# Low parts of the out-projection's weights on VectorE, and products of zeros ahead of RWKV's products with an inverse

## The chip, the cores and the metric

The kernel runs on one core of one Trainium2 chip, in one launch. The time is device microseconds of one execution of the whole program. The kernel before takes 2244.4 us, the median of 3 runs (2242.67 to 2246.63). Engine names in rows: PE is TensorE's products and PEld its weight loads, DVE is VectorE, ACT is ScalarE, POOL is GpSimd, SP is SyncE, which here only issues transfers.

## What is computed

Two layers of a hybrid mixer over 1280 tokens (256 of context, 1024 of a picture), width 1024. Each layer normalises its input, projects it, runs four mixers on 256 channels each, joins their outputs, projects them back and adds the result, normalised and gated, to the input:

```python
def mixer_layer(h, mod, p, grid, init, need_out):
    shift, scale, gate = jnp.split(mod, 3, axis=-1)
    hn = rmsnorm(h, p['norm_pre']) * (1.0 + scale) + shift
    proj = hn @ p['w_in']
    f_rw, f_s5, f_ssd, f_gla = split_last(proj, [RW_COLS, S5_COLS, SSD_COLS, GLA_COLS])
    ...
    y = jnp.concatenate([y_rw, y_s5, y_ssd, y_gla], axis=-1).astype(h.dtype) @ p['w_out']
    return h + gate * rmsnorm(y, p['norm_post']), states
```

The RWKV mixer is a recurrence in both directions over a 64x64 state per head (4 heads):

```python
def step(S, inp):
    r_t, w_t, k_t, v_t, kk_t, a_t = inp
    sa = jnp.einsum('bhvk,bhk->bhv', S, -kk_t)
    S = S * w_t[:, :, None, :] + sa[..., None] * (kk_t * a_t)[:, :, None, :] + v_t[..., None] * k_t[:, :, None, :]
    y = jnp.einsum('bhvk,bhk->bhv', S, r_t) if need_out else None
    return S, y
```

The S5 mixer is a diagonal complex recurrence; SSD and GLA are chunked linear attention.

## The kernel before

`body` runs two layers. For each it calls `project` (norm, the input projections, GLA and SSD), then `rw` (RWKV, with the jobs of S5 and the last six input projections put in between), then `out_proj`. The context tokens need no output in the second layer.

**RWKV.** The recurrence is done in windows of 128 tokens, 10 windows, two halves of 64 tokens in each, and both directions at once (a unit u is a direction and a pair of heads, two heads side by side on the free axis). Inside a half the dependence of a token on those before it is a triangular system, and its inverse TT is worked out ahead: `rw_inv` solves 32x32 blocks on VectorE (r_N, r_X, r_tp) and joins them by small products on TensorE (pi<-r_DN, r_DT, r_Bb, r_Rb). `rw_chain` is the serial part. In each half it clears a PSUM bank X (px) with a product of zeros (r_z, bf16), adds the products of A with the values and of the state (r_S) with r_AR, copies the upper half of X to r_rs (left columns on VectorE, right ones on ACT, L1374 and L1375), multiplies by the inverse into the bank pu (four products pu<-r_rs,r_TT), copies the result to r_UV, and forms the new state from pu<-r_UV,r_Bt (X2), which VectorE adds to the decayed old state. `rw_out` forms the outputs r_yw, and `rw_final` norms and gates them (r_yt) and writes them to the scratch tensor yd. The five stages of a window stand in the program in the order 3, 2, 4, 1, 0 (`ORDER`), each for another window, and a scheduler that simulates a time line (L1823) sets the order of the instructions on each engine from that. PSUM has 8 banks in this stage: px 2, pb 2, and one each for pu, pi, ps and p (S5). Since pu has a single bank, the product with the inverse, the copy out of it, X2 and the read of X2 follow each other.

**Out-projection.** The weights (8 blocks m of 128 outputs, each 128x1024 in fp32) are split by `split` into a high part, a cast to fp32r on ACT (L1551, o_w0h to o_w7h), and a low part, the rest, by a subtraction (helper `tt`, L342; o_w0l to o_w7l). It goes in 16 halves of 128x512 through a ring of two buffers o_w: SP issues the transfer of a half (L1550), ACT casts it, and the engine named by the last argument (v for VectorE, p for POOL) subtracts; then the buffer is free for the next transfer. The argument is `"pv"[m % 2]` (L1656), so even blocks go to POOL. Then blocks of 256 tokens follow: their inputs o_y come from yd by SP, are split likewise (o_yh, o_yl), and for each pair of m TensorE does 48 products of 128x256 into one bank pj; ACT squares the bank (o_acc, o_sq), VectorE copies it to o_o (L1681), POOL sums the squares, and a norm, the gate (VectorE) and the input o_x (VectorE and POOL in turn) end the block. SP issues o_w, o_y and o_x from one queue, in order.

Of the kernel before, what the change touches and what calls it, by code (L numbers as in the profile page):

```python
# [24 lines left out]
KD = D // 128  # L25
# [218 lines left out]

RN = (3, 2, 10)
NF = 2

WB = (4, 4)
G1 = ("misc gk", "misc gk")
# [8 lines left out]
class K:  # L258
# [1093 lines left out]
    def rw_chain(self, W, S):  # L1352
        nc = self.nc
        A, AR, Bt, TT, UV, PM = [W[n] for n in ("A", "AR", "Bt", "TT", "UV", "PM")]
        w, need = W["w"], W["need"]
        if need:
            yw = W["yw"] = self.R("r_yw", [128, 2, 256], 1)
        hs = [slice(64 * h, 64 * h + 64) for h in range(2)]
        for s in range(2):
            last = w == 9 and s == 1  # L1360
            X = self.P("px").rearrange("p (u f) -> p u f", u=4)
            self.mm(X.rearrange("p u f -> p (u f)"), self.zero[:, 0:128], self.zero, True, False)
            for u in range(4):
                for h in range(2):
                    self.mm(X[0:64, u, hs[h]], A[:, s, u, h, 0:64], UV[:, s, u, hs[h]], False, False)
            if S is not None:
                for u in range(4):
                    ar = AR[:, u // 2, u % 2, s]
                    if need:
                        self.mm(X[:, u], ar.rearrange("p k t -> p (k t)"), S[:, u], False, False)  # L1370
                    else:
                        self.mm(X[0:64, u], ar[:, 0], S[:, u], False, u == 3)
            rs = self.rzero("r_rs", [128, 4, 128], 2)
            nc.vector.tensor_copy(rs[0:64, :, 0:64], X[0:64, :, 0:64])  # L1374
            nc.scalar.copy(rs[64:128, :, 64:128], X[0:64, :, 64:128])  # L1375
            ps = self.P("pu")[0:64].rearrange("p (u v) -> p u v", u=4)
            for u in range(4):
                self.mm(ps[:, u], TT[:, s * 4 + u], rs[:, u])
            nc.vector.tensor_copy(UV[0:64, s, 0:2], ps[:, 0:2])  # L1379
            nc.scalar.copy(UV[0:64, s, 2:4], ps[:, 2:4])  # L1380
            Sn = None
            if not last:
                X2 = self.P("pu").rearrange("p (u f) -> p u f", u=4)
                for u in range(4):
                    self.mm(X2[:, u], Bt[:, s, u], UV[:, s, u])

                Sn = self.rzero("r_S", [128, 4, 128], 2)
                for h in hs:
                    if S is None:
                        nc.vector.tensor_copy(Sn[h, :, h], X2[h, :, h])  # L1390
                    else:
                        self.tt(Sn[h, :, h], S[h, :, h], PM[h, s].unsqueeze(2).to_broadcast([64, 4, 64]), OP.mult, EG["sp"])
                        self.tt(Sn[h, :, h], X2[h, :, h], Sn[h, :, h], OP.add)
            if need:
                for u in range(4):
                    for h in range(2):
                        self.mm(X[64:128, u, hs[h]], A[:, s, u, h, 64:128], UV[:, s, u, hs[h]], False, u == 3 and h == 1)
                for d in range(2):
                    o = yw[64:128, s] if d == 0 else yw[0:64, s]
                    nc.scalar.copy(o, X[64:128, 2 * d:2 * d + 2].rearrange("p u f -> p (u f)"))  # L1400
            S = Sn
        return S
# [23 lines left out]
    def rw_final(self, blocks):  # L1426
# [3 lines left out]
        bs = sorted(blocks)  # L1430
        x = self.R("r_fin", [128, 2, 6, 128], NF)
        for i, b in enumerate(bs):
# [214 lines left out]
    def out_proj(self, l, h, dst, hi=None, lo=None):  # L1647

        nc, mg = self.nc, self.md[l, 1]
        self.where.update({f"o_w{m}{s}": "oa" if m < 4 else "ob" for m in range(8) for s in "hl"}, o_w="oa",  # L1650
                          **{n: "oy" for n in ("o_yh", "o_yl", "o_y")}, **{n: "oo" for n in ("o_o", "o_acc", "o_sq", "o_x")})
        W = []
        for m in range(8):
            W.append([x.rearrange("p (k m) -> p k m", k=KD) for x in self.split("o_w", f"o_w{m}", [128, 1024], 1, self.A["wout"][l, m], "pv"[m % 2])])
        nb = 1 if hi else 2
        for b in (0, 2, 3, 1, 4) if hi else (2, 3, 1, 4):  # L1656
            b0 = b * 256
            j = 1 if b == 0 else 0
            yh, yl = [self.R("o_y" + s, [128, KD, 256], nb, F32R) for s in "hl"]
            for g in range(4):  # L1660
                gs = slice(2 * g, 2 * g + 2)
                y = self.R("o_y", [128, 2, 256], 3)
                nc.sync.dma_start(out=y, in_=self.yd[l][g * 256:(g + 1) * 256, b0:b0 + 256].rearrange("(k p) t -> p k t", p=128))
                nc.scalar.copy(yh[:, gs], y)
                self.tt(yl[:, gs], y, yh[:, gs].bitcast(F32), OP.subtract)
            x = self.R("o_x", [128, KD, 256])
            nc.sync.dma_start(out=x, in_=h[:, b0:b0 + 256].rearrange("(k p) t -> p k t", p=128))
            o = self.R("o_o", [128, KD, 256], 2)
            acc = self.R("o_acc", [128, 2, 256], 2)
            for m in range(0, 8, 2):  # L1670
                ps = self.P("pj")
                for q in range(2):
                    wh, wl = W[m + q]
                    i = 0
                    for w, t in ((wh, yh), (wl, yh), (wh, yl)):
                        for k in range(KD):
                            self.mm(ps[:, q * 256:(q + 1) * 256], w[:, k], t[:, k], i == 0, i == 3 * KD - 1)
                            i += 1
                sq = acc if m == 0 else self.R("o_sq", [128, 2, 256], 2)
                self.act(sq.rearrange("p k t -> p (k t)"), ps, AF.Square)  # L1680
                nc.vector.tensor_copy(o[:, m:m + 2].rearrange("p k t -> p (k t)"), ps)  # L1681
                if m:
                    self.tt(acc, acc, sq, OP.add, "pppv"[m // 2])
            rs = self.norm([acc[:, 0], acc[:, 1]], "pn")
            od = dst(b0, 256).rearrange("(k p) t -> p k t", p=128)
            for m in range(0, 8, 2):
                for q in range(2):
                    self.stt(o[:, m + q], o[:, m + q], mg[:, m + q, j:j + 1], rs, OP.mult, OP.mult)
                self.tt(o[:, m:m + 2], o[:, m:m + 2], x[:, m:m + 2], OP.add, RA[m // 2])
                if m % 4 == 2:  # L1690
                    nc.sync.dma_start(out=od[:, m - 2:m + 2], in_=o[:, m - 2:m + 2])
            if hi:
                md = self.md[l + 1, 0]
                acc = self.R("o_acc", [128, 2, 256], 2)
                for m in range(0, 8, 2):
                    sq = acc if m == 0 else self.R("o_sq", [128, 2, 256], 2)
                    self.act(sq, o[:, m:m + 2], AF.Square)
                    if m:
                        self.tt(acc, acc, sq, OP.add, AA[m // 2])
                rs = self.norm([acc[:, 0], acc[:, 1]], "pn")  # L1700
                bb = 0 if b == 0 else (b + 1) // 2
                t = b0 - BLK[bb][0]
                for k in range(KD):
                    self.stt(o[:, k], o[:, k], md[:, 8 + k, j:j + 1], rs, OP.mult, OP.mult)
                    ho, lw = [v[bb][:, k, t:t + 256] for v in (hi, lo)]
                    self.act(ho, o[:, k], AF.Identity, bias=md[:, k, j:j + 1])
                    self.stt(lw, o[:, k], md[:, k, j:j + 1], ho.bitcast(F32), OP.add, OP.subtract)
# [119 lines left out]
```

## Time and profile before

| What | Value |
| --- | --- |
| Median of 3 runs | 2244.4 us (2242.67 to 2246.63) |
| Profiled execution | 2243.13 us |
| Its span (first to last instruction) | 2241.4 us |
| Mean granted clock of TensorE | 0.926 of full speed |
| RWKV, layer 0 | 700 to 1045 us of the span |
| RWKV, layer 1 | 1757 to 2085 us |
| RWKV's last rows and out-projection, layer 0 | 1045 to some 1210 us |
| RWKV's last rows and out-projection, layer 1 | 2085 us to the end |

The profile is one execution, and the rows below are of it; its time is 1.3 us below the median of the runs. Busy shares are of the whole span and hide that the stages differ: a window of the trace is read for itself. [...]

### The profile page before, as it was taken

Reading aid. Unit: us, or ns where it says so; the run is one execution under the profiler, and the core shown is the slowest. Engines: PE = TensorE matmul, PEld = TensorE weight load, DVE = VectorE, ACT = ScalarE, POOL = GpSimd, SP = SyncE. Lnnn points to the kernel's source line nnn. Section 1 sums busy time; section 2 is a strip of 40 time slices with the busy share of each in tenths; the row PEclk is TensorE's granted clock in tenths of the full one; section 3 lists DMA queues with packets and bytes.
Section 4 is the critical chain, followed back from the end, with each engine's and each line's share of the span. In section 5 each row is a group of like instructions: output and inputs, shape, how many; then the busy total and the mean of one; then the engine's idle time right before and its main releaser. Section 6 shows DMA issues by size and latency. Waiting matters only on the chain. (4 is left out here: it accounts for less than half of the span.)

```text
span 2241.4 us, 45148 instructions
## 1 busy us (share of the span) xinstructions
PE 1947.4 (87%) x17712; PEld 1664.7 (74%) x17712; DVE 1529.2 (68%) x3423; ACT 916.7 (41%) x2009; POOL 846.5 (38%) x965
## 2 busy tenths in 40 slices
PE   6777999999997887878799779999999787889697
PEld 4667889678886676765799667887888676676497
DVE  3877646794146888885377786677754899896344
ACT  2434314333256447632233544234335755544220
POOL 0446460342024455532322255522332454542222
PEclk9889999999998888979999899999999989889698
DMA  7234425434633222214333335242234232212332
GB/s 247 74 118 132 157 83 170 128 115 133 187 99 116 88 74 81 70 40 140 90 114 113 120 125 175 89 145 80 70 112 125 98 105 68 86 47 73 122 104 95
DMA packets 204021, 246.83 MB, mean 110 GB/s; under 512 B 28384, under 2 KB 145632, under 8 KB 203808
## 3 DMA queue, kind: packets, MB, share of 16 engines
q1 hardware_dynamic: 169936, 213.13, 30.6%
q10 hardware_dynamic: 33008, 28.45, 3.9%
q8 instruction: 139, 2.28, 0.4%
q0 software_dynamic: 864, 2.36, 0.3%
q14 instruction: 74, 0.61, 0.1%
HBM read 169.27 MB, written 76.71 MB: 110 GB/s over the span
## 5 line engine op out<-in xcount | busy, mean ns | idle before, releaser
L330 PE MATMUL pj<-hi,i_wh 128*128 128x512 f32 (+1 forms) x696 | 180.2, 379 | 18.3 <-DVE hi L1528 13.2
L330 PE MATMUL pj<-lo,i_wh 128*128 128x512 f32 (+1 forms) x696 | 176.9, 372 | 0.1
L330 PE MATMUL pj<-hi,i_wl 128*128 128x512 f32 (+1 forms) x696 | 174.3, 368 | 2.7 <-DVE i_wl L342 2.7
L342 DVE TENSOR_TENSOR i_wl<-i_w,i_wh 128x512 fp32r<-128x512 f32 x108 | 84.8, 791 | 107.6 <-ACT i_wh L1551 37.6
L330 PEld LDWEIGHTS pj<-hi,i_wh 128*128 128x128 f32 x696 | 124.2, 199 | 43.1 <-DVE hi L1528 13.4
L330 PEld LDWEIGHTS pj<-hi,i_wl 128*128 128x128 f32 x696 | 123.9, 195 | 25.6 <-DVE i_wl L342 3.2
L330 PEld LDWEIGHTS pj<-lo,i_wh 128*128 128x128 f32 x696 | 124.0, 197 | 22.6 <-issue 2.6
L330 PE MATMUL px<-r_UV,r_A 128*64 128x64 f32 x1216 | 108.2, 247 | 17.0 <-DVE r_UV L1379 9.8
L330 PEld LDWEIGHTS px<-r_UV,r_A 128*64 128x64 f32 x1216 | 92.6, 157 | 37.5 <-DVE r_UV L1379 13.9
L1551 ACT CAST i_wh<-i_w 128x512 fp32r<-128x512 f32 x108 | 66.0, 620 | 122.0 <-PE pj L330 80.8
L1289 DVE TENSOR_TENSOR r_X<-r_X,r_tp 128x30 f32<-128x30 f32 (+1 forms) x300 | 93.8, 313 | 8.0
L342 DVE TENSOR_TENSOR r_tp<-r_N,r_X 128x30 f32<-128x30 f32 (+1 forms) x300 | 90.5, 302 | 7.2
L330 PE MATMUL pb<-r_AD,r_BK 128*128 128x256 f32 x320 | 85.2, 407 | 5.5 <-POOL r_BK L342 3.6
L342 POOL TENSOR_TENSOR r_S<-r_S,r_PM 64x256 f32<-64x256 f32 x72 | 54.0, 750 | 79.0 <-DVE r_S L342 66.8
L342 DVE TENSOR_TENSOR r_A<-pb,rcon 128x512 f32<-128x512 f32 x80 | 53.5, 682 | 42.2 <-PE pb L330 41.9
L330 PEld LDWEIGHTS pb<-r_AD,r_BK 128*128 128x128 f32 x320 | 60.9, 201 | 17.1 <-POOL r_BK L342 3.9
L330 PE MATMUL pj<-i_wh,hi 128*128 128x256 f32 x448 | 71.0, 296 | 2.9 <-ACT i_wh L1551 1.5
L345 POOL TENSOR_SCALAR r_AD<-r_AR 64x512 f32<-64x512 f32 (+1 forms) x80 | 54.4, 680 | 48.9 <-PE pb L330 42.4
L330 PE MATMUL pu<-r_rs,r_TT 128*64 128x128 f32 x320 | 49.2, 303 | 21.1 <-ACT r_rs L1375 20.8
L342 POOL TENSOR_TENSOR o_o<-o_o,o_x 128x512 f32<-128x512 f32 x18 | 23.8, 1323 | 114.7 <-DVE o_o L348 113.5
L330 PE MATMUL pj<-i_wl,hi 128*128 128x256 f32 x448 | 66.8, 289 | 0.2 <-DVE i_wl L342 0.2
L330 PEld LDWEIGHTS pj<-i_wh,hi 128*128 128x128 f32 x448 | 61.4, 198 | 6.7 <-issue 2.7
(469 smaller groups left out, 5445.9 us busy)
## 6 DMA issues: line engine op xcount, KB each, us to landing
i_w<-in_win SPq DMA_DIRECT2D x108, 256.0 KB, 3.0
r_in<-rm SPq DMA_DIRECT2D x36, 512.0 KB, 4.5
a_w<-in_ada SPq DMA_DIRECT2D x64, 256.0 KB, 3.8
rm<-i_o SPq DMA_DIRECT2D x48, 256.0 KB, 2.5
o_y<-yd SPq DMA_DIRECT2D x36, 256.0 KB, 3.0
i_o<-in_ada SPq DMA_DIRECT2D x32, 256.0 KB, 4.6
z_st<-s5t SPq DMA_DIRECT2D x32, 256.0 KB, 2.7
o_w<-in_wout SPq DMA_DIRECT2D x32, 256.0 KB, 2.7
```

The costliest lines, as they stand in the source:

```text
L330: self.nc.tensor.matmul(out, lhsT, rhs, start=start, stop=stop, skip_group_check=True)
L342: (self.nc.vector if e == "v" else self.nc.gpsimd).tensor_tensor(out, a, b, op)
L345: (self.nc.vector if e == "v" else self.nc.gpsimd).tensor_scalar(out, a, s1, s2, op0, op1)
L1289: last = nc.vector.tensor_tensor(X[:, :, :i, r0:4], X[:, :, :i, r0:4], tmp[:, :, :i, r0:], OP.add)
L1551: self.nc.scalar.copy(hi[:, v], w)
```

## The change

It does two things. The call of `split` in `out_proj` loses its last argument, so that all low parts of the out-projection's weights go to `split`'s default engine, VectorE: 8 more subtractions of 128x512 in each layer (o_w0l, o_w2l, o_w4l and o_w6l, two halves each). In `rw_chain`, four products of zeros (the bf16 tile r_z as weights and as 512 columns) are written into the bank of pu ahead of the four products with the inverse, each of which begins a new sum, so that nothing of the zeros is left. There are 20 halves in each layer, so 160 such products, each with its load of weights.

```diff
--- before.py
+++ after.py
@@ -244,6 +244,8 @@
 
 RN = (3, 2, 10)
 NF = 2
+
+FILL = 4
 
 WB = (4, 4)
 G1 = ("misc gk", "misc gk")
@@ -1373,7 +1375,11 @@
             rs = self.rzero("r_rs", [128, 4, 128], 2)
             nc.vector.tensor_copy(rs[0:64, :, 0:64], X[0:64, :, 0:64])
             nc.scalar.copy(rs[64:128, :, 64:128], X[0:64, :, 64:128])
-            ps = self.P("pu")[0:64].rearrange("p (u v) -> p u v", u=4)
+            bank = self.P("pu")
+
+            for _ in range(FILL):
+                self.mm(bank, self.zero[:, 0:128], self.zero)
+            ps = bank[0:64].rearrange("p (u v) -> p u v", u=4)
             for u in range(4):
                 self.mm(ps[:, u], TT[:, s * 4 + u], rs[:, u])
             nc.vector.tensor_copy(UV[0:64, s, 0:2], ps[:, 0:2])
@@ -1651,7 +1657,7 @@
                           **{n: "oy" for n in ("o_yh", "o_yl", "o_y")}, **{n: "oo" for n in ("o_o", "o_acc", "o_sq", "o_x")})
         W = []
         for m in range(8):
-            W.append([x.rearrange("p (k m) -> p k m", k=KD) for x in self.split("o_w", f"o_w{m}", [128, 1024], 1, self.A["wout"][l, m], "pv"[m % 2])])
+            W.append([x.rearrange("p (k m) -> p k m", k=KD) for x in self.split("o_w", f"o_w{m}", [128, 1024], 1, self.A["wout"][l, m])])
         nb = 1 if hi else 2
         for b in (0, 2, 3, 1, 4) if hi else (2, 3, 1, 4):
             b0 = b * 256
```

The lines of the kernel after stand 2 to 6 lower. The scheduler puts many other instructions of the RWKV stages in another order. Three places follow.

On TensorE, in the second half of a window in layer 0 (r_S is the state, r_AR what it is multiplied by, r_AD, r_BK, r_DN and r_Am belong to the next window's blocks and inverse, z_ and p_ to S5; a number behind a name is its buffer's). Before:

```order
L330 MATMUL px<-r_S_7029,r_AR_8211 128x128 x4
L330 MATMUL pi<-r_DN,r_Am 32x32 x24
L1263 MATMUL pb<-con,r_BK 128x128 x8
L330 LDWEIGHTS r_z
L330 MATMUL px<-r_z 128x512
L330 MATMUL ps<-rcon,r_yw 128x128 x2
L330 MATMUL p_9891<-z_us,z_st 128x160 x3
L330 MATMUL pu<-r_rs_7012,r_TT_6837 64x128 x4
```

After:

```order
L332 MATMUL px<-r_S_7033,r_AR_8235 128x128 x4
L332 LDWEIGHTS r_z
L332 MATMUL pu<-r_z 128x512
...
L332 LDWEIGHTS r_z
L332 MATMUL pu<-r_z 128x512
L332 LDWEIGHTS r_z
L332 MATMUL px<-r_z 128x512
L332 MATMUL ps<-rcon,r_yw 128x128 x2
L332 MATMUL pb<-r_AD_6322,r_BK 128x256 x4
...
L332 MATMUL pi<-r_DN,r_Am 32x32 x8
L332 MATMUL pu<-r_rs_7012,r_TT_6837 64x128 x4
```

The four zeros into pu come right after the state's product, and other work that stood between the state's product and the product with the inverse is now partly behind it.

On VectorE, at the end of RWKV and the start of the out-projection in layer 1 (r_yt are RWKV's gated outputs). Before:

```order
L348 SCALAR_TENSOR_TENSOR r_yt<-r_yt,par,r_ks_18041 128x2x128 x2
L342 TENSOR_TENSOR o_w1l<-o_w,o_w1h 128x512 x2
L342 TENSOR_TENSOR o_w3l<-o_w,o_w3h 128x512
L1681 COPY o_o<-pj 128x512
L342 TENSOR_TENSOR o_w3l<-o_w,o_w3h 128x512
L1681 COPY o_o<-pj 128x512
L342 TENSOR_TENSOR o_w5l<-o_w,o_w5h 128x512 x2
```

After:

```order
L350 SCALAR_TENSOR_TENSOR r_yt<-r_yt,par,r_ks_18121 128x2x128 x2
L344 TENSOR_TENSOR o_w0l<-o_w,o_w0h 128x512 x2
L344 TENSOR_TENSOR o_w1l<-o_w,o_w1h 128x512 x2
L1687 COPY o_o<-pj 128x512
L344 TENSOR_TENSOR o_w2l<-o_w,o_w2h 128x512 x2
L344 TENSOR_TENSOR o_w3l<-o_w,o_w3h 128x512 x2
L344 TENSOR_TENSOR o_w4l<-o_w,o_w4h 128x512 x2
L1687 COPY o_o<-pj 128x512
L344 TENSOR_TENSOR o_w5l<-o_w,o_w5h 128x512 x2
```

o_w0l stands directly behind r_yt, and o_w2l and o_w4l behind the copies out of pj. In layer 0 the order is o_w0l, o_w1l, the first half of o_w2l, a copy out of pj, its second half, and so on by turns.

On ACT, the same place in layer 1 (o_acc<-pj is the Square of the first two blocks of outputs). Before:

```order
L1551 CAST o_w0h<-o_w 128x512 x2
L1551 CAST o_w1h<-o_w 128x512 x2
L1551 CAST o_w2h<-o_w 128x512 x2
L1551 CAST o_w3h<-o_w 128x512
L339 ACTIVATE o_acc<-pj 128x512
L1551 CAST o_w3h<-o_w 128x512
```

After:

```order
L1557 CAST o_w0h<-o_w 128x512 x2
L1557 CAST o_w1h<-o_w 128x512 x2
L341 ACTIVATE o_acc<-pj 128x512
L1557 CAST o_w2h<-o_w 128x512 x2
L1557 CAST o_w3h<-o_w 128x512 x2
```

The Square now stands ahead of both casts of o_w2h, and before it stood between the casts of o_w3h.

## Rows read from the trace of the kernel before

**Rows 1.** The page, busy time, share of the span and instructions of each engine:

```profile
PE 1947.4 (87%) x17712; PEld 1664.7 (74%) x17712; DVE 1529.2 (68%) x3423; ACT 916.7 (41%) x2009; POOL 846.5 (38%) x965
```

**Rows 2.** Windows, RWKV stages: stretch, us, busy (instructions) by engine, clock, DMA, GB/s:

```profile
700.00:1045.00 345.00, 284.15 (x3488) 237.14 (x3487) 290.89 (x647) 180.40 (x433) 159.82 (x213) 0.88 0.27 85
1757.00:2085.00 328.00, 271.36 (x3412) 224.92 (x3412) 282.37 (x635) 176.57 (x428) 158.16 (x211) 0.90 0.27 82
```

**Rows 3.** Windows, layer 0's 13 stretches at the low clock, one and their sum:

```profile
815.00:819.00 4.00, 3.49 (x16) 3.16 (x17) 3.90 (x11) 2.09 (x6) 1.93 (x3) 0.57 0.00 0
...
sum 80.00, PE 65.72 PEld 55.50 DVE 66.53 ACT 30.69 POOL 23.45; mean PE 5.06 PEld 4.27 DVE 5.12 ACT 2.36 POOL 1.80
```

**Rows 4.** Windows, the 13 such stretches of layer 1, their sum:

```profile
sum 61.00, PE 54.92 PEld 46.63 DVE 50.85 ACT 18.33 POOL 19.73; mean PE 4.22 PEld 3.59 DVE 3.91 ACT 1.41 POOL 1.52
```

**Rows 5.** Windows, the 4 us ahead of the one stretch shown:

```profile
811.00:815.00 4.00, 0.25 (x3) 0.06 (x1) 3.97 (x6) 0.00 (x0) 2.44 (x6) 1.00 0.53 171
```

**Rows 6.** Chain of waits, 2100 to 2145 us: start, us, what:

```profile
2107.16 1.68 DVE r_yt L348 x4
...
2112.00 2.30 POOL o_w0l L342 x2
2114.31 4.11 DMA o_w<-in_wout
...
2123.37 0.63 ACT o_w2h L1551
...
2124.07 1.29 POOL o_w2l L342
...
2139.54 2.67 DMA o_w<-in_wout
...
2142.98 18.90 PE pj L330 x144
```

**Rows 7.** Tile o_w: duration in ns min/median/max, first and last start, forms:

```profile
L342 DVE TENSOR_TENSOR o_w1l<-o_w,o_w1h x4: 692/693/693, 1076.4 to 2123.3; 128x512 fp32r<-128x512 f32 x4
...
L342 DVE TENSOR_TENSOR o_w7l<-o_w,o_w7h x4: 676/780/1340, 1102.5 to 2149.9; 128x512 fp32r<-128x512 f32 x4
```

**Rows 8.** Timeline, layer 0's out-projection: start, us, engine, what [idle before <-releaser]:

```profile
1067.73 0.88 DVE L348 SCALAR_TENSOR_TENSOR r_yt<-r_yt,par,r_ks 128x256 f32<-128x256 f32 x2
1068.74 1.26 POOL L342 TENSOR_TENSOR r_yt<-r_yt,r_fin 128x512 f32<-128x512 f32 x1 [8.09 <-DVE r_yt L348]
...
1071.79 2.50 POOL L342 TENSOR_TENSOR o_w0l<-o_w,o_w0h 128x512 fp32r<-128x512 f32 x2
1073.09 1.55 SPq L1550 DMA_DIRECT2D o_w<-in_wout  x2
...
1104.27 0.62 ACT L1551 CAST o_w7h<-o_w 128x512 fp32r<-128x512 f32 x1 [1.85 <-DMA o_w<-in_wout]
```

**Rows 9.** Timeline, SP in layer 1's out-projection:

```profile
2112.81 1.40 SPq L1663 DMA_DIRECT2D o_y<-yd  x3
...
2115.29 0.53 SPq L1550 DMA_DIRECT2D o_w<-in_wout  x1
```

**Rows 10.** Timeline, TensorE: products of zeros and the next, full and low clock:

```profile
1876.90 0.38 PE L330 MATMUL px<-r_z 128*128 128x512 bf16 x1
1877.12 0.61 PE L330 MATMUL ps<-rcon,r_yw 128*128 128x128 f32 x4
...
1998.77 0.63 PE L330 MATMUL px<-r_z 128*128 128x512 bf16 x1
1999.19 0.93 PE L330 MATMUL ps<-rcon,r_yw 128*128 128x128 f32 x4
```

**Rows 11.** Tile r_rs: engines idle before its instructions until (us, times):

```profile
  ACT r_rs L1375: 45.0, 30
```

**Rows 12.** Timeline, TensorE: products with an inverse:

```profile
815.51 1.97 PE L330 MATMUL pu<-r_rs,r_TT 128*64 128x128 f32 x8 [4.26 <-ACT r_rs L1375]
...
2059.14 1.09 PE L330 MATMUL pu<-r_rs,r_TT 128*64 128x128 f32 x8
```

## The prediction

> **What bounds the kernel now.** I read the busy shares first, then the busy time of the two RWKV stretches by windows, then the chain of waits. Over the whole span TensorE is the busiest engine, 87% [rows 1], but that mean hides two kinds of stage. In the RWKV stages (700 to 1045 us in layer 0, 1757 to 2085 us in layer 1, 673 us together) VectorE is the fuller one, 290.89 of 345 and 282.37 of 328 us, and TensorE's granted clock is 0.88 and 0.90 [rows 2]. There the reader is to see what VectorE does where the clock is low. I marked the pieces, to 1 us, in which the clock stood at its lower level: 13 in layer 0, 80 us together, and 13 in layer 1, 61 us. VectorE is busy for 66.53 us of the 80 and 50.85 of the 61 [rows 3, 4], 83% in both; in the rest of the stretches it is 224.4 of 265 and 231.5 of 267, or 85% and 87%. So a slow TensorE hardly slows VectorE. The other way round it shows: from 811 to 815 VectorE works 3.97 of 4 us and TensorE 0.25, at full clock [rows 5]; the next 4 us are at 0.57 [rows 3]. TensorE waits, and its clock falls.
>
> The second kind of stage is the start of each out-projection. The chain of waits runs there through a ring of two 128x512 buffers for the weights: transfer, cast, low part, next transfer. In layer 1 it passes RWKV's last VectorE rows, then POOL's o_w0l at 2112.00, then transfer by transfer to 2142.98, and from there on only TensorE products [rows 6].
>
> **The low parts.** Sixteen subtractions, eight in each layer, leave POOL for VectorE. One takes 0.69 us there (o_w1l) [rows 7]; on POOL the pair takes 2.50 [rows 8], 1.25 each. What counts first is the start. In layer 0 the casts of o_w0h are long done and VectorE ends r_yt at 1067.73 + 0.88 = 1068.6, but POOL has its own r_yt product and its transfers to issue and begins o_w0l at 1071.79; only after its first half SP issues the next weight transfer, 1073.09 [rows 8]. In the new order o_w0l stands on VectorE right behind r_yt: halves done at about 1069.4 and 1070.1 against 1073.0 and 1074.3, 3.6 and 4.2 us earlier. Then each of o_w2, o_w4 and o_w6 shortens a turn of the ring by 1.29 [rows 6] - 0.69 = 0.60 us, 1.8 us for three. Against this, the second half of o_w2l, o_w4l and o_w6l now stands behind a copy out of PSUM that waits for products and for ACT's Square; with TensorE starting 3.6 us earlier too I price this at 0.5. Layer 0: -4.2 - 1.8 + 0.5 = -5.5 us.
>
> In layer 1 VectorE ends r_yt at 2107.16 + 1.68 = 2108.8 and POOL starts at 2112.00 [rows 6]. The third weight transfer moves ahead of a load of o_y and can go at 2109.6 instead of 2114.31, 4.7 us earlier. The fourth stays behind that o_y, which waits for RWKV's result to land and is issued at 2112.81; so it goes at 2113.3 instead of 2115.29, 2.0 earlier [rows 6, 9]. On ACT the Square of the first two outputs now stands ahead of both casts of o_w2h, and it needs the products of o_w1's second half: 2113.3, a transfer of 2.7 to 4.1 us (2.67 and 4.11 in the chain), cast and low 1.3, some 4 us of products at the low clock, Square 0.6: casts of o_w2h from about 2122.7, against 2123.37 (0.7 earlier). The turns of o_w2 and o_w4 give 0.6 each, and the two halves then come closer together than before: 3 us at o_w6, where TensorE takes over the chain. Layer 1: -3 us.
>
> Both: -8.5 us. The ends are -2.3 and -10.7. The upper one: -6.0 and -4.7, nothing lost behind the copies. The lower one: layer 1 gives nothing, because the Square and the copies eat it (VectorE's queue then holds o_w3l and o_w4l behind a late copy), and layer 0 only its 3.6 less 1.26 for POOL's r_yt product, which runs at the same moment. That overlap has a price in the trace: an o_w7l that runs beside POOL's o_acc takes up to 1.34 us against 0.69 [rows 7].
> [...]
>
> **The products of zeros.** 40 products with an inverse get four products of 128x512 ahead of them, 160 in all, each with its weight load. The trace has the same product (r_z into px): the next one starts 0.22 us later at full clock (1876.90 to 1877.12) and 0.42 at the low one [rows 10]. 160 x 0.22 = 35 us of TensorE time, 67 at the most. Cover: TensorE is idle 117 of the 673 us [rows 2], and 45.0 us of this in front of this very product, in 30 waits for the copies of r_rs [rows 11]. The order puts them only partly there: in the second half of a window they stand between r_S's product and the copies, where they replace other products as filler; in the first half they run before X is made. Their bank is the single pu, free once VectorE has read X2; r_S's product needs that read too, so I add no wait. Ends: 0 and +35 us. VectorE, the pace-setter, idles 99.8 of 673 us, 15%, and only there can TensorE be late for it: 0.15 x 35 = +5.
>
> What they give is the clock. Were the slow pieces cured, VectorE would gain at most its idle time in them, 13.5 + 10.1 = 23.6 us; if only the idle above the usual rate goes, 1.3 + 2.0 = 3.3 us [rows 2 to 4]. I count the pieces that begin within 2 us of the start of such a product: 10 of 26, one at 815 (product at 815.51, after 4.26 us of waiting), the last at 2061 (2059.14) [rows 12]. 10/26 x 23.6 = -9. The other sixteen begin in waits for the 32x32 inverse or for S5, where no zeros stand. So -9 + 5 = -4 us.
>
> The change also puts other RWKV, S5 and second-layer projection products in another order; they are the same instructions, and I count 0 for it, with 8 us to either side (a twelfth of VectorE's idle time).
>
> **Sum.** -8.5 - 4 = -12.5. The profiled execution took 2243.1 us (span 2241.4 and 1.7 around it), so 2230.6; the median of the runs lies 1.3 above it: 2232 us, -0.55%. What is late next in the RWKV stages is VectorE's own work; in the out-projections TensorE from the last weight on.
>
> **Rivals.**
> The zeros hold the clock. For it: in each fall the trace shows TensorE waiting just before [rows 5, 12]. Against: most falls lie where no zeros are put. All slow pieces gone: -23.6 + 5 - 8.5 = -27, 2217 us.
> [...]
>
> The zeros only cost nothing and give nothing. VectorE's equal shares in slow and fast pieces speak for it. -8.5: 2236 us.
>
> Slower: the zeros stand in TensorE's queue, which runs in order, ahead of what VectorE waits for. Place: the first half of a window, where they come ahead of the inverse's products and of the next X. For it: 0.9 us per group at full clock, 1.7 at the low one; against: TensorE's idle time. If half of the 35 us arrives at VectorE and the clock gains nothing, +17.5 - 8.5 = +9, 2253 us; all of it, 2271. It decides from a quarter of the 35 us on.
>
> The low parts don't do what they say: on VectorE they queue behind the copies and beside POOL's products, the ring keeps its pace (-2), and the RWKV stages balance: 2242 to 2244 us.
>
> **How the numbers follow.** Forecast 0.37, clock held 0.17, only the low parts 0.13, slower 0.22, no effect 0.11. The forecast's own range is 2222 to 2242 (its bounds and the 8 us of order). With the rivals to either side, and leaving out 1 in 10 at each end, 2212 to 2256. A measurement of this kernel tells about 0.2%, 4.5 us, from no change. Faster by more: 0.35 of the forecast, 0.17, 0.10 and 0.02, 0.64. Within it: 0.02 + 0.03 + 0.02 + 0.07 = 0.14. Slower: 0.22.
>
> **What would show it.** Right: o_w0l on VectorE within 0.2 us of r_yt's end, the last o_w7h cast in layer 0 some 5 us sooner after r_yt than the 36.5 us of before (1067.73 to 1104.27 [rows 8]); in layer 1 the products taking over about 3 us sooner after r_yt; granted clock 0.92 or more in the RWKV stages with VectorE's busy time unchanged and the stages shorter by a few us. Wrong: a clock near 1.0 with the stages much shorter (the clock did bind); the clock up and the stages as long (VectorE binds alone); waits of VectorE for pu, pi or px that grow (the zeros are in the way); o_w2l waiting for copies so long that the ring is no faster.

## The result and the profile after

The kernel after takes 2258.09 us (median of 5 runs, 2254.97 to 2262.58), the kernel before 2244.4 us (median of 5, 2242.67 to 2249.12). The ratio is 1.0055, 95% interval 1.0037 to 1.0074: 0.55% or some 14 us slower, where 0.55% faster was forecast. The profiled execution took 2262.58 us, 4.5 above its median, so its stages carry a little more than the median's loss.

The page's busy times of the kernel after, as in [rows 1]:

```profile
PE 1985.3 (88%) x17872; PEld 1689.0 (75%) x17872; DVE 1535.1 (68%) x3439; ACT 917.3 (41%) x2009; POOL 821.0 (36%) x949
```

TensorE is busy 38 us longer. For the loss that is a wrong trail, as the experiments show; the next rows say where the time went. They are windows from the first copy of r_rs in a layer to the end of its last r_yt, the RWKV stage without its overlap into the stages beside it (columns as in [rows 2]). First the kernel before:

```profile
704.50:1068.60 364.10, 296.33 (x3556) 245.81 (x3554) 296.64 (x673) 182.91 (x439) 161.44 (x211) 0.87 0.27 83
1761.30:2108.80 347.50, 281.68 (x3440) 231.17 (x3440) 287.99 (x659) 178.67 (x431) 157.79 (x210) 0.88 0.26 80
```

and the kernel after:

```profile
704.70:1086.00 381.30, 315.29 (x3631) 256.03 (x3629) 298.59 (x673) 182.86 (x439) 160.04 (x211) 0.87 0.25 76
1781.50:2130.80 349.30, 294.46 (x3516) 238.70 (x3516) 284.24 (x657) 179.73 (x431) 154.22 (x207) 0.89 0.25 79
```

Layer 0's stage is 17.2 us longer, layer 1's 1.8. VectorE does the same work in both (296.64 and 298.59, 287.99 and 284.24 us); what has grown is the time in which it stands, from 67.5 to 82.7 and from 59.5 to 65.1 us, 20.8 together. The granted clock of the stages is what it was. Where VectorE stands is told by the groups of its instructions (busy, mean ns, then the idle time just before them and what ended it). Before:

```profile
L1278 DVE STREAM_TRANSPOSE r_N<-r_Ad 128x1024 f32<-128x1024 f32 x20 | 39.7, 1985 | 12.3 <-ACT r_Ad L1035 12.2
L342 DVE TENSOR_TENSOR r_S<-pu,r_S 64x256 f32<-64x256 f32 x72 | 30.1, 419 | 11.0 <-PE pu L330 9.8
L1379 DVE COPY r_UV<-pu 64x256 f32<-64x256 f32 x40 | 16.4, 410 | 9.9 <-PE pu L330 9.8
```

After:

```profile
L1280 DVE STREAM_TRANSPOSE r_N<-r_Ad 128x1024 f32<-128x1024 f32 x20 | 39.9, 1995 | 21.4 <-ACT r_Ad L1037 21.3
L344 DVE TENSOR_TENSOR r_S<-pu,r_S 64x256 f32<-64x256 f32 x72 | 30.3, 421 | 24.9 <-PE pu L332 23.6
L1385 DVE COPY r_UV<-pu 64x256 f32<-64x256 f32 x40 | 16.4, 410 | 11.0 <-PE pu L332 10.8
```

The copy r_UV is the first that waits for the product behind the zeros, and its wait hardly grows (9.9 to 11.0 us). The waits that grew stand one step later: the new state r_S (+13.9 us) and the next window's transpose r_N (+9.1). The longest single wait for r_S is in layer 0, in the seventh half. VectorE's timeline there, after:

```profile
824.06 2.44 DVE L344 TENSOR_TENSOR z_x<-z_b,z_t 64x636 f32<-64x636 f32 x3
826.53 0.42 DVE L1385 COPY r_UV<-pu 64x256 f32<-64x256 f32 x1
...
827.32 1.60 DVE L344 TENSOR_TENSOR r_BK<-r_th,r_cs 128x512 f32<-128x512 f32 x1
828.84 0.63 DVE L1311 STREAM_TRANSPOSE r_DN<-r_DT 128x256 f32<-128x256 f32 x1
832.98 0.87 DVE L344 TENSOR_TENSOR r_S<-pu,r_S 64x256 f32<-64x256 f32 x2 [3.50 <-PE pu L332]
```

and the same half before, where the copy r_UV starts at 818.33:

```profile
820.50 2.63 DVE L342 TENSOR_TENSOR z_x<-z_a,z_bb 64x636 f32<-64x636 f32 x3
...
823.68 1.16 DVE L348 SCALAR_TENSOR_TENSOR r_a<-r_a,r_in 128x256 f32<-128x256 f32 x2
824.76 2.43 DVE L342 TENSOR_TENSOR z_x<-z_b,z_t 64x636 f32<-64x636 f32 x3
827.22 0.88 DVE L342 TENSOR_TENSOR r_S<-pu,r_S 64x256 f32<-64x256 f32 x2
```

Before, z_x (S5) and r_a (another window) lie between r_UV and r_S and cover the wait. After, z_x has been done ahead of r_UV, and VectorE runs dry for 3.50 us. The product that r_S waits for has moved too. TensorE there, after:

```profile
826.60 0.87 PE L332 MATMUL p<-z_x,z_st 128*128 128x160 f32 x2 [3.22 <-DVE z_x L344]
...
829.40 1.27 PE L332 MATMUL p<-z_x,z_st 128*128 128x160 f32 x4
830.60 1.12 PE L332 MATMUL px<-r_UV,r_A 128*64 128x64 f32 x8
831.65 1.29 PE L332 MATMUL pu<-r_UV,r_Bt 128*128 128x128 f32 x8
```

and before:

```profile
820.37 1.16 PE L330 MATMUL pu<-r_UV,r_Bt 128*128 128x128 f32 x8 [0.24 <-ACT r_UV L1380]
...
823.23 0.51 PE L330 MATMUL p<-z_x,z_st 128*128 128x160 f32 x2 [1.10 <-DVE z_x L342]
```

S5's products p, which themselves wait for z_x (3.22 us), now stand ahead of the state's product pu<-r_UV,r_Bt and hold it to 831.65; before, it came first. No zeros stand in this piece: it is the same work in another order.

The out-projections, layer 0, timeline of the kernel after (VectorE, POOL, SP, ACT; compare [rows 8]):

```profile
1085.17 0.88 DVE L350 SCALAR_TENSOR_TENSOR r_yt<-r_yt,par,r_ks 128x256 f32<-128x256 f32 x2
1085.96 1.29 DVE L344 TENSOR_TENSOR o_w0l<-o_w,o_w0h 128x512 fp32r<-128x512 f32 x2
...
1086.18 2.22 POOL L344 TENSOR_TENSOR r_yt<-r_yt,r_fin 128x512 f32<-128x512 f32 x1 [8.09 <-DVE r_yt L350]
...
1086.67 0.93 SPq L1556 DMA_DIRECT2D o_w<-in_wout  x2
1087.70 0.38 SPq L1673 DMA_DIRECT2D o_x<-in_hT  x1
1090.90 1.25 SPq L1556 DMA_DIRECT2D o_w<-in_wout  x2
...
1097.26 0.62 ACT L1557 CAST o_w2h<-o_w 128x512 fp32r<-128x512 f32 x1 [6.53 <-DMA o_w<-in_wout]
...
1124.03 0.62 ACT L1557 CAST o_w7h<-o_w 128x512 fp32r<-128x512 f32 x1 [3.61 <-DMA o_w<-in_wout]
```

The start is as forecast: o_w0l right at r_yt's end, the next weights out at 1086.67, 1.5 us behind r_yt's start against 5.4 before. But the 1024 KB of o_x went out long ahead of the ring before:

```profile
1053.99 0.38 SPq L1667 DMA_DIRECT2D o_x<-in_hT  x1
```

Now it goes out at 1087.70, between the weights; the half issued at 1090.90 is cast at 1097.26, 6.4 us later. The last o_w7h stands 38.9 us behind r_yt (36.5 before) in this execution. POOL's r_yt, beside o_w0l, takes 2.22 us against 1.26, 0.96 us more, with 1.07 us of o_w0l still to run at its start.

Layer 1, the chain of waits, after (compare [rows 6]):

```profile
2138.32 9.22 DMA o_w<-in_wout
...
2161.78 8.33 PE pj L332 x66
```

Again a half of the weights, queued behind o_x and two o_y, takes 9.22 us (in this layer o_x stood among the weights before, too, at 2114.77). TensorE takes over 30.9 us behind the last r_yt (which ends at 2130.8; before 34.1), so 3.2 us sooner, about the forecast's 3. How far these two figures carry is seen under e1.

### The profile page after: what moved, and what is told of

It reads as the page before. It is cut to its first block, busy times and chain, and to the rows that moved or that the text cites. A ratio compares the mean times of both kernels' runs of the same rounds, so it can differ in the third digit from the quotient of the medians.

```text
span 2260.6 us, 45461 instructions
## 1 busy us (share of the span) xinstructions
PE 1985.3 (88%) x17872; PEld 1689.0 (75%) x17872; DVE 1535.1 (68%) x3439; ACT 917.3 (41%) x2009; POOL 821.0 (36%) x949
## 5 line engine op out<-in xcount | busy, mean ns | idle before, releaser
L332 PE MATMUL pj<-hi,i_wh 128*128 128x512 f32 (+1 forms) x696 | 180.4, 380 | 16.7 <-DVE hi L1534 13.2
L332 PE MATMUL pj<-hi,i_wl 128*128 128x512 f32 (+1 forms) x696 | 173.8, 366 | 2.7 <-DVE i_wl L344 2.7
L344 DVE TENSOR_TENSOR i_wl<-i_w,i_wh 128x512 fp32r<-128x512 f32 x108 | 90.6, 844 | 112.6 <-ACT i_wh L1557 52.9
L344 DVE TENSOR_TENSOR r_tp<-r_N,r_X 128x30 f32<-128x30 f32 (+1 forms) x300 | 96.3, 321 | 7.3
L344 POOL TENSOR_TENSOR o_acc<-o_acc,o_sq 128x512 f32<-128x512 f32 x23 | 31.1, 1352 | 116.0 <-ACT o_sq L341 115.9
```

The source lines that it names most:

```text
L332: self.nc.tensor.matmul(out, lhsT, rhs, start=start, stop=stop, skip_group_check=True)
L344: (self.nc.vector if e == "v" else self.nc.gpsimd).tensor_tensor(out, a, b, op)
```

## The experiments

All are compared with the kernel before on the same chip. They ask whether the zeros' time costs the 14 us or the new order, what the low parts are worth and why so little, and what makes an order good.

**e1, the low parts alone.**

```diff
- ... self.split("o_w", f"o_w{m}", [128, 1024], 1, self.A["wout"][l, m], "pv"[m % 2]) ...
+ ... self.split("o_w", f"o_w{m}", [128, 1024], 1, self.A["wout"][l, m]) ...
```

> The low parts alone: the kernel before, with o_w0l, o_w2l, o_w4l and o_w6l on VectorE and no products of zeros; RWKV of layer 0 keeps the order of before. Theory A (the recorded sum of the out-projections was right and the loss is all in RWKV): -8.5 us, 2236. Theory B (in the profile after, layer 0's out-projection takes 148.5 us from RWKV's last r_yt on, against 144.4 before, because the new order of SP's queue puts the 1 MB load of o_x at 1087.70 between the halves of the weights, and the o_w issued next takes 6.33 us to land against 2.5 to 2.8 before; layer 1 gains about 3): layer 0 +2 to +4, layer 1 -3, 2242 to 2246, and o_x again among the first weights.

Measured: 2243.78 us (12 runs), ratio 1.0006 (0.9988 to 1.0023). No gain: theory A's -8.5 us lies outside the interval (-3 to +5 us), and no loss is shown either. SP's queue in layer 0, and the chain in layer 1:

```profile
1067.11 0.38 SPq L1667 DMA_DIRECT2D o_x<-in_hT  x1
```

```profile
2115.58 8.92 DMA o_w<-in_wout
...
2143.07 6.94 PE pj L330 x56
```

o_x is again among the first weights. The last o_w7h of layer 0 stands 35.5 us behind r_yt (before 36.5), and in layer 1 TensorE takes over 35.0 us behind it (before 34.1). For the same low parts, the traces of after and e3 have 38.9 and 34.2 in layer 0 and 30.9 and 32.9 in layer 1; for the low parts as before, e2 and e4 have 37.8 and 37.8, and 32.1 and 33.7. From trace to trace each figure moves by 1 to 5 us, so neither the 2.4 us that after loses in layer 0 nor the 3.2 us that it gains in layer 1 is shown to come from the edit.

This edit, too, changes an order: in layer 0's RWKV it is before's, in layer 1's it is another, and that stage is 5.1 us longer in the profile (352.6 against 347.5). So e1 is not the price of the low parts alone.

**e2, the zeros alone,** the kernel after with the low parts put back:

```diff
- ... self.split("o_w", f"o_w{m}", [128, 1024], 1, self.A["wout"][l, m]) ...
+ ... self.split("o_w", f"o_w{m}", [128, 1024], 1, self.A["wout"][l, m], "pv"[m % 2]) ...
```

> The products of zeros alone, four ahead of each product with an inverse, low parts as before; RWKV of layer 0 in the order of after. If the low parts are worth -8.5 us, this is slower than after by so much: 2267. If they are worth about nothing (theory B of the low parts), it is as after: 2256 to 2260, with layer 0's RWKV some 17 us longer than before (368.6 us from 700 to the last r_yt) and layer 1's some 2 us.

Measured: 2256.97 us (6 runs), ratio 1.0062 (1.0042 to 1.0082). The whole loss comes with the edit of the zeros.

**e3, the order of after without the zeros.** A function changes the program after the scheduler has set the order; of each four products one is left (of the 160 in all, 43), and that of one column:

```diff
+ ...
+ if i.outs[0].memref == bank and i.sync_info is None and made[at].sync_info is None:
+     del made[at]          # the load; the product is skipped
+     continue
+ ...
+ i = copy.replace(i, ins=(x, i.ins[1]), outs=(y,))   # x, y: one column of 512
```

> The kernel after with every engine's instructions in its own order, but of each four products of zeros only one is left, and that of one column instead of 512: the order of after without the zeros' time (117 products and their loads fewer). Theory 1 (the zeros' time stands on the path, 160 x 0.22 us = 35 us of TensorE, of which 19 came through): layer 0's RWKV loses its 17 us and the whole is 2240 to 2244. Theory 2 (the new order of RWKV, S5 and projections costs it, and the zeros' time is hidden in TensorE's idle time): within 4 us of after, 2254 to 2260, and a clock somewhat lower than after's 0.922.

Measured: 2260.65 us (6 runs), ratio 1.0071 (1.0049 to 1.0093), as slow as after itself. The zeros' time is not what costs. In the trace every engine has after's order in both RWKV stages. The windows and VectorE's groups of e3:

```profile
705.90:1086.70 380.80, 301.12 (x3576) 249.88 (x3574) 298.86 (x673) 182.58 (x439) 159.69 (x211) 0.87 0.24 76
1780.70:2129.40 348.70, 282.02 (x3460) 234.15 (x3460) 284.18 (x657) 179.14 (x431) 155.06 (x207) 0.86 0.25 79
```

```profile
L1281 DVE STREAM_TRANSPOSE r_N<-r_Ad 128x1024 f32<-128x1024 f32 x20 | 39.9, 1995 | 23.6 <-ACT r_Ad L1038 23.6
L345 DVE TENSOR_TENSOR r_S<-pu,r_S 64x256 f32<-64x256 f32 x72 | 30.2, 420 | 25.6 <-PE pu L333 24.3
L1386 DVE COPY r_UV<-pu 64x256 f32<-64x256 f32 x40 | 16.3, 408 | 8.7 <-PE pu L333 8.5
```

TensorE's busy time is back to 301 and 282 us, and the stages are as long as after's, with the same two waits grown. With the zeros some of the clock goes, too: over the whole span the granted clock is 0.9155 (median of the runs; 0.910 to 0.918), against 0.923 in e2 and in after (0.920 to 0.927). So e3 and e4 price the zeros' time together with the clock that they give.

**e4, the order of before with the zeros,** put in after the order was set:

```diff
+ ...
+ for _ in range(n):      # ahead of the first product with r_rs into a bank
+     made.append(copy.replace(ld, name=nc.get_next_instruction_name(), sync_info=None))
+     made.append(copy.replace(mm, ..., sync_info=None, outs=(o,), stop_tensor_calc=True))
```

> The kernel before with every engine's instructions in its own order, and four products of zeros with their loads put directly ahead of each product with an inverse: the zeros' time without the new order. Theory 1 (the zeros' time): 12 to 20 us slower than before, 2256 to 2264. Theory 2 (the order): within 4 us of before, 2240 to 2248; if the zeros lift the clock and that counts, below 2240.

Measured: 2247.27 us (12 runs), ratio 1.0013 (0.9998 to 1.0027). Theory 2 holds: the zeros in before's order (which the trace shows in both stages) cost 3.5 us at the middle, not told from none. The wait of r_UV, which stands behind them:

```profile
L1380 DVE COPY r_UV<-pu 64x256 f32<-64x256 f32 x40 | 16.4, 410 | 23.2 <-PE pu L331 23.0
```

13 us more than before. This is the longest execution of the 12, 2256.09 us, 8.8 above their median, so the row shows more than the usual price. Its granted clock in the two stages is 0.88 and 0.87, but of the 12 it has the lowest clock over the whole span, and before's profile (0.926) one of the highest of its kernel: the 12 have 0.925 to 0.935 (median 0.930), and the kernel before has 0.917 to 0.927 in 22 of its 23 runs (median of all 0.922). So four products of zeros do lift the clock, by some 0.008 in the mean over the whole span, here and in after's order, and no time is seen to come of it.

**e5, the low parts with o_x late.**

```diff
...
+ with self.tc.issue_after(self.wd.ins):      # wd: the last transfer of o_w
      nc.sync.dma_start(out=x, in_=h[:, b0:b0 + 256].rearrange("(k p) t -> p k t", p=128))
```

> The low parts on VectorE, no zeros, and each block's load of o_x queued on SP behind the last o_w; the order of RWKV is that of the low parts alone. Theory B (the 1 MB of o_x beside the weights ate the gain): in layer 0 the seventh o_w transfer goes out some 9 to 10 us after the last r_yt instead of 12.5, in layer 1 some 14 to 15 instead of 17.9, and the whole is 6 us faster than the low parts alone, 2238. Rival (the ring is held by the copies out of PSUM and the products, not by o_x): 2242 to 2246, with the same issue times as before.

Measured: 2237.13 us (12 runs), ratio 0.9976 (0.9962 to 0.9990): 5.7 us under the kernel before on its chip, where e1 was level with it. In the traces e1 and e5 have the same order of RWKV in both layers. Theory B holds. It is the one version that beats both kernels. SP's queue in layer 0:

```profile
1068.31 29.85 SPq L1550 DMA_DIRECT2D o_w<-in_wout  x14
1098.21 0.43 SPq L1668 DMA_DIRECT2D o_x<-in_hT  x1
```

the last cast of layer 0:

```profile
1100.57 0.62 ACT L1551 CAST o_w7h<-o_w 128x512 fp32r<-128x512 f32 x1 [3.15 <-DMA o_w<-in_wout]
```

and the chain in layer 1:

```profile
2125.60 2.81 DMA o_w<-in_wout
...
2137.57 12.44 PE pj L330 x102
```

The halves of the chain land in 2.6 to 2.8 us from there on, with no 8.92 among them. The last o_w7h of layer 0 stands 33.8 us behind r_yt, and in layer 1 TensorE takes over 27.8 us behind it (2109.8), 3.1 sooner than after and 6.3 sooner than before. Both are below every figure named under e1.

**o6, o5 and o8: other orders, without zeros.** The low parts are as before, and the zeros are taken out as in e3.

```diff
-FILL = 4
+FILL = 6          # o5: 5, o8: 8; o1 and o2 below: 1 and 2
```

> Low parts as before; the order that the scheduler makes with six products of zeros per product with an inverse, and then the zeros taken out as in e3 (one of one column is left). Theory S (what VectorE has queued between its copy of r_UV and r_S sets the time: where it is less than the 3.5 us of the longest wait for r_S in the profile after, VectorE stands; the lack, summed over the 38 places with durations of before's rows, is 19.5 us in before's order and 29.7 in after's, which e3 shows to be 15 us slower, 1.5 us for each us of lack): here the lack is 17.1, so -3.5 us, 2240. Rival (any order other than before's costs some 13 us): 2257.

> As o6, with the order that five products of zeros make. Theory S: the lack is 21.0 us, +2 us, 2246. Rival (any other order costs 13): 2257.

> As o6, with the order that eight products of zeros make. Theory S: the lack is 27.1 us, +11 us, 2255. Rival (any other order costs 13): 2257. A second rival, that the order's cost is a matter of chance and the lack says nothing of it: the three orders stand in another row than 17.1, 21.0, 27.1.

Measured: o6 2286.32 us, ratio 1.0189 (1.0167 to 1.0211); o5 2264.79, 1.0097 (1.0080 to 1.0115); o8 2274.40, 1.0148 (1.0125 to 1.0171). Theory S falls: the order with the least lack is the slowest. What VectorE has queued ahead of r_S is one such place among several: in o6 it stands 13.4 us for r_S and 29.3 for r_N (before 11.0 and 12.3):

```profile
L1281 DVE STREAM_TRANSPOSE r_N<-r_Ad 128x1024 f32<-128x1024 f32 x20 | 39.7, 1987 | 29.3 <-ACT r_Ad L1038 29.3
L345 DVE TENSOR_TENSOR r_S<-pu,r_S 64x256 f32<-64x256 f32 x72 | 30.2, 419 | 13.4 <-PE pu L333 12.1
```

**o1 and o2: the orders of one and two.** Is it the zeros' planned time, or any other order?

> As o6: low parts as before, the order that one product of zeros per product with an inverse makes, and the zeros taken out (one of one column left). The orders of four, five, eight and six were 15, 22, 32 and 43 us slower than before's. Theory D (the scheduler plans for the zeros' time, and its plan is worse the more of it there is): one product moves little, 0 to +5 us, 2243 to 2248. Theory L (the order is a draw: any small cause makes another one, and before's is a good one): as likely +10 to +40 as with more, 2253 to 2283.

> As o1, with the order that two products of zeros make. Theory D: +3 to +9 us, 2246 to 2252, between one and four. Theory L: +10 to +40, in no row with the number of zeros.

Measured: o1 2261.17 us, ratio 1.0076 (1.0049 to 1.0104); o2 2277.04, 1.0136 (1.0110 to 1.0163). Theory D falls: one planned product costs as much as four, and two more.

**e6, o_x late alone,** e5 with the low parts by turns again:

```diff
- ... self.split("o_w", f"o_w{m}", [128, 1024], 1, self.A["wout"][l, m]) ...
+ ... self.split("o_w", f"o_w{m}", [128, 1024], 1, self.A["wout"][l, m], "pv"[m % 2]) ...
```

> Low parts on POOL and VectorE by turns as before, no zeros, each block's o_x queued behind the last o_w. If the gain of the low parts with o_x late (5.7 us) comes from o_x alone: 2237 to 2239. If the two belong together (layer 0's o_x was early in before, so that only layer 1 can gain, some 3 us): 2239 to 2242.

Measured: 2263.76 us, ratio 1.0080 (1.0056 to 1.0104). Neither was expected. Layer 0's stage is as before; layer 1's, which was put in another order by this edit, is 24.4 us longer, at a clock of 0.81 (before 0.88):

```profile
1759.10:2131.00 371.90, 296.45 (x3440) 244.53 (x3440) 291.15 (x659) 180.17 (x431) 158.81 (x210) 0.81 0.24 75
```

This edit has nothing to do with RWKV or zeros. It moved the order of RWKV all the same, and the kernel is slower than with the change under study. How much of the 24.4 us the lower clock makes, no run separates. In its out-projections the last o_w7h of layer 0 stands 38.0 us behind r_yt, and in layer 1 TensorE takes over 32.3 us behind it: without the low parts the late o_x is not seen to bring anything.

**e7, twelve zeros in the order of before:**

```diff
-    zeros_in(nc, 4)
+    zeros_in(nc, 12)
```

> As e4 (before's order, low parts as before) with twelve products of zeros instead of four ahead of each product with an inverse: 480 x 0.22 us = 106 us of TensorE. e4 measured +3.5 us for four. If that is the zeros' own price and grows with their number: +10 us, 2253. If they are free only as long as they fit into the wait for r_rs (45.0 us in 40 places, 1.1 each, and four take 0.9): twelve take 2.6, 1.5 more than the wait, 60 us more in the chain, up to 2303 where VectorE has nothing else to do, and about +10 where it is covered by VectorE's other work as the rest of TensorE's waits is (15%). The granted clock in the RWKV stages, 0.87 in before and 0.88 and 0.86 in e4, rises clearly if zeros hold it, above 0.92.

Measured: 2285.03 us, the median of five runs (a sixth took 3755.03 us and is left out), ratio 1.0176 (1.0147 to 1.0206). Its windows and its r_UV:

```profile
701.40:1090.30 388.90, 335.66 (x3776) 257.80 (x3794) 292.39 (x673) 183.08 (x439) 161.78 (x211) 0.92 0.25 77
1784.70:2152.40 367.70, 321.82 (x3660) 245.57 (x3678) 290.44 (x659) 178.93 (x431) 158.45 (x210) 0.92 0.24 76
```

```profile
L1380 DVE COPY r_UV<-pu 64x256 f32<-64x256 f32 x40 | 16.6, 415 | 62.1 <-PE pu L331 62.0
```

Now the zeros are paid for: r_UV waits 62.1 us against 9.9, and the kernel is 39.9 us slower, between the two figures expected. The clock rises from 0.87 and 0.88 to 0.92, at the edge of what was expected of zeros that hold it; over the whole span it is 0.937, about as far above e4's 0.930 as e4 is above before.

All the profiles together, by the same windows; idle is the stretch less VectorE's busy time, both layers:

| Kernel | RWKV 0, us | VectorE busy | RWKV 1, us | VectorE busy | idle, both | median to before |
| --- | --- | --- | --- | --- | --- | --- |
| before | 364.1 | 296.6 | 347.5 | 288.0 | 127.0 | |
| e1, e5 (order of before in layer 0) | 364.2, 362.1 | 297.0, 296.4 | 352.6, 353.1 | 288.6, 287.7 | 131.2, 131.1 | 0.0, -5.7 |
| e4 (order of before, zeros) | 368.8 | 295.7 | 356.0 | 289.5 | 139.6 | +3.5 |
| after | 381.3 | 298.6 | 349.3 | 284.2 | 147.8 | +13.7 |
| e2, e3 (order of after) | 376.6, 380.8 | 296.7, 298.9 | 351.2, 348.7 | 284.6, 284.2 | 146.6, 146.5 | +13.2, +16.9 |
| o1, o2 | 368.6, 377.9 | 298.2, 296.0 | 363.7, 362.5 | 288.4, 287.7 | 145.7, 156.6 | +16.0, +31.9 |
| o5, o6, o8 | 371.6, 381.9, 374.6 | 294.6, 297.1, 300.0 | 358.9, 363.9, 367.0 | 289.6, 290.7, 286.7 | 146.3, 158.0, 154.9 | +22.0, +43.5, +31.6 |
| e6 | 362.7 | 296.4 | 371.9 | 291.2 | 147.0 | +18.6 |
| e7 | 388.9 | 292.4 | 367.7 | 290.4 | 173.8 | +39.9 |

VectorE's busy time lies between 292 and 300 us in layer 0 and between 284 and 291 in layer 1 in all fourteen. The stage is that work plus what VectorE stands. That is so of any engine, and ACT's busy time is as steady (181 to 184 and 178 to 181 us), so this alone doesn't make VectorE the one that sets the pace; it is the fuller of the two. The last two columns go together, with two marks against reading them to the microsecond: a row is one execution (e4's profiled one, 2256.09 us, was the longest of its 12), and the orders of e5 and o1 to o8 also differ outside these stretches.

## Why the prediction was wrong

**The step that failed** is the one on the order: "they are the same instructions, and I count 0 for it, with 8 us to either side (a twelfth of VectorE's idle time)". It cost 13 us by the median of e2 (with the zeros) and 17 by that of e3 (all but without them; interval +11 to +21 us), and 20.8 us of VectorE's idle time in the profile of after. VectorE was rightly read as the fuller engine, with the same work in any order and 15% idle time. What was missing is that this idle time depends on what else stands in its queue when a product is late; the same instructions in another order added a sixth to it (127.0 to 147.8). The mechanism is shown at the one place above; the measure of it that was tried (theory S) failed. The bound of 8 us rested on no row.

**The rival "slower"** named nearly the right time, 2253 us, for the wrong reason. It let TensorE's zeros arrive late at VectorE. e3 takes them away and nothing comes back; e4 puts them in and pays 3.5 us. Its mechanism exists (e7: with twelve products r_UV waits 62.1 us and the kernel is 39.9 us slower), but with four it doesn't decide (e4, +3.5 us). Its sign, that VectorE's waits for pu grow, did come, for r_S by 13.9 us, and would have misled: they grow as much in e3.

**The zeros,** +5 us for their time and -9 for the clock, -4 in all: e4 has both and +3.5 (interval -0.4 to +6 us), so the -4 is missed. The two terms are not measured apart. The clock does rise, by some 0.008 in the mean over the whole span with four products and 0.015 with twelve (e7), but in neither run does it give back more than the zeros' time takes; the step from a count of slow pieces to a share of VectorE's idle time is not borne out. That TensorE waits just before "each fall" holds in before's trace for 25 of the 26, with 0.9 us of waiting or more in the 5 us before; the one at 2061 comes after 14 us in which TensorE is busy throughout (windows of 1 us from 2047 to 2061, 1.00 each, at a clock of 1.00; the next two have 0.65 and 0.50). The cover was misread, too. The 45.0 us, 30 times, of [rows 11] count weight loads and products, which wait for the same copies:

```profile
  PEld pu L330: 24.2, 18
  PE pu L330: 20.8, 12
```

The products themselves wait 20.8 us, 12 times, less than the 35 us of the zeros; in e4 11.6 us of this wait are left. (VectorE's idle time is 99.7 us, not 99.8, which changes nothing.)

**The low parts,** -8.5 us: e1 measured none (-3 to +5 us), with layer 1's RWKV in an order that is 5.1 us longer in the profile. After's own trace has the early starts that were forecast, 3.6 to 4.2 us in layer 0; by the end of the ring they are not told from the scatter between traces (e1). The 1.26 us that the end of -2.3 takes off for POOL's r_yt no run shows on VectorE: beside it o_w0l's halves take 0.683 to 0.690 us (after), and it is POOL's r_yt that takes 0.96 us more. What the sum left out is o_x: in layer 0 it moved in SP's queue to a place between the weights, in layer 1 it stood there already, and the sum looked only at o_y. e5, with o_x behind the weights, is 5.7 us faster, and its two out-projections are 2.7 us (33.8 against 36.5) and 6.3 us sooner, 9 in all. That this is near the forecast's 8.5 is luck: layer 0 gave half of its 5.5, layer 1 twice its 3, and 3.1 of that are o_x's by the trace of after. That the median shows 5.7 of the 9 fits the order of layer 1's RWKV, 5.6 us longer than before's; this was not tested.

**Open.** What makes one order better than another is not settled. r_S, r_N, r_A and r_UV all take their turn as the place where VectorE runs dry, and the one measure tried (theory S) failed. The clock is a rival that no run excludes for the other orders: without zeros, o1 to o8 and e6 have 0.909 to 0.915 over the whole span by the medians, before 0.921 and 0.922, and either the clock makes their stages longer or the longer waits make the clock lower. For after's order it is not the cause: e2 and after have before's clock and are 13 and 14 us slower. What a faster clock would be worth without the zeros' time, no run here shows. Of the orders run, before's has the shortest stage in layer 1 and, but for e5's and e6's runs of the same order, in layer 0, each by one profile.

## What to carry to other kernels

Where a scheduler sets the order, an edit changes two things, and the second can be many times the first: to price an edit, separate them, by putting the work in after the order is fixed, and by taking it out of the new one. In a stage whose pace-setter is an engine with many short waits, look at what work it has queued behind each of them, though no reading of it here foretold a time; "the same instructions in another order" has no bound there but a measured one. And where a ring of small loads feeds the critical stage, look at every large load in the same issue queue: here an early start brought 0.0 us by the median with one of them in between (e1), and 5.7 us with it behind the ring (e5).

## What was not expected of the hardware

A half of the weights (256 KB) lands in 2.7 us by the median of before's 32 and in 2.6 to 2.8 us in the chain of e5 from 2125.60 on, but took 6.4 us to its cast behind the 1024 KB of o_x in layer 0 of after, and 9.22 (after) and 8.92 us (e1) behind o_x and two o_y in layer 1. And products of zeros do count for the clock: in before's order the granted clock over the whole span is 0.922 without them, 0.930 with four per inverse and 0.937 with twelve.
